# First projection of a hybrid decoder layer: four weight units run side by side by k tiles, weights fetched by pairs of k tiles, squares on ScalarE, and constant matmuls on TensorE before the input arrives

## The chip, the core and the metric

One core of one Trainium2 chip runs the whole kernel in one launch. The engines are named as the profile names them: PE is TensorE's matmul and PEld its weight load, DVE is VectorE, ACT is ScalarE, POOL is GpSimd, and SP is SyncE, which here only issues transfers. The metric is device microseconds (us) of one execution, as the median of several.

## What is computed

One decoder layer over 512 positions of width 1024. The part that the change touches is the start: the RMS norm of x and the first quarter of the combined input projection, the forget logits of the HGRN2 heads (512 columns, four heads of 128).

```python
h = rms_norm(x, norm_mix[l])            # x is (1, 512, 1024) f32
proj = h @ w_in[l]                      # (1024, 3584) weights
hq, hf, hi, hg, mq, mk, mv = jnp.split(proj, IN_SPLITS, axis=-1)
o_hgrn = hgrn2_mixer(hq, hf, hi, hg, lb_table[l], hgrn_norm[l])
# in it: f = lb + (1 - lb) * sigmoid(hf); log f is summed along chunks of 32 positions
```

After it come block-sparse attention, the output projection, cross-attention, a squared-ReLU MLP and a final norm.

## The kernel before, in words

**Precision.** Every operand of a large product is split in two: ACT copies it to a rounded part (`hi`, type fp32r), DVE subtracts that from the original (`lo`), and PE adds three products, hi·hi, hi·lo and lo·hi. A weight of 128 x 1024 values is a unit: `wr` is its raw tile (three buffers), `wh` and `wl` its two parts (`split_raw`, line 246). x is held transposed, as eight k tiles of 128 rows by 512 positions: `xraw` raw, `xhi` and `xlo` the parts, scaled by the norm's gain from `vec` (`split_x`, line 494). The division by the root of the mean square comes later: DVE and ACT square and add the k tiles (`square_x`, line 503, tiles `xsq`, `Sx`, `Sy`), PE sums that over partitions (`nr`), and ACT makes `rb1` of it, by which the finished products are multiplied.

**Tiling of the first projection.** Units 0 to 3 are the four heads of hf; a unit holds all eight k tiles of one head. PE (lines 595 to 610) goes through the k tiles once for heads 0 and 1 together (48 matmuls of 128 x 512), then once for head 2 and once for head 3 (24 each). So the first pass needs a new k tile of x every six matmuls, and the two weights whole. Each head has an accumulator bank from the pool `pacc` of four banks; another pool, `pside`, has four for everything else.

**What sets the order.** Down to line 607 each engine's instructions stand as the code writes them (`manual_schedule`); behind it the framework's scheduler places them, and side work (the norm's column sums `nc`, the HGRN2 steps) is put between matmuls by a planner, `Pace` (line 37), that adds up assumed costs. `need(u)` (line 315) splits units two ahead of use and loads them up to six ahead, as raw buffers come free.

**Queues.** SP issues the transfers of x and the weights one after the other; `vec` goes over ACT's queue. A transfer's issue waits when the eighth one before it has not landed, since eight semaphores are used in turn.

**What follows.** Stage hi (units 4 to 7, token by token, `tm_stage`) uses x again and all four banks of `pacc`; then come hq (units 8 to 11) and the HGRN2 work. `ev_f` (line 588) takes hf out of its banks with rb1, sigmoids follow, then the logarithm `lnf`, its chunk sums `b` (a scan on DVE), and their exponentials `eb` and `kt` on ACT. `Vh` is hi scaled, on ACT; it frees the banks that hq takes.

Of the kernel before, what the change touches and what calls it, by code (L numbers as in the profile page):

```python
# [122 lines left out]
def hybrid_layer(ctx: ExitStack, tc: tile.TileContext, xT, memT, ws, vecs, consts, rots, out):  # L123
    nc = tc.nc
    pace = Pace()
    V, A, PE = (pace.engine(e, t) for e, t in ((nc.vector, "dve"), (nc.scalar, "act"), (nc.tensor, "pe")))
    SY, PO = pace.engine(nc.sync, "dma"), pace.engine(nc.gpsimd, "pool")
# [8 lines left out]
    ordered = tc.manual_schedule()  # L136
# [33 lines left out]
    raws, his, los, late, n8 = {}, {}, {}, [], [1]  # L170
    state = {"load": 0, "split": 0}
# [74 lines left out]
    def split_raw(u, raw, a, b, eng=None):  # L246
        A.activation(his[u][:, a:b], raw[:, a:b], AF.Copy)

        def lower(hi=his[u], lo=los[u]):
            (eng or V).tensor_sub(lo[:, a:b], raw[:, a:b], hi[:, a:b].bitcast(F32))  # L250
        later(lower)

    def split_part(u, a, b, eng=None):
        split_raw(u, raws[u], a, b, eng)

    def split_begin():
        u = state["split"]
        his[u] = wpool.tile([P, D], F32R, tag="whi", name=f"wh{u}", bufs=WBUFS)
        if u < MLP - 4 and u % 4 == 0:
            los[u] = ep.tile([P, D], F32R, tag="wloe", name=f"wl{u}", bufs=1)  # L260
        else:
            los[u] = wpool.tile([P, D], F32R, tag="wlo", name=f"wl{u}", bufs=WBUFS - 1)
        state["split"] += 1
        return u

    def split_unit(eng=None):
        u = split_begin()
        split_part(u, 0, D, eng)
        del raws[u]
# [18 lines left out]
    def f1_prep(j, s):  # L288

        split_raw(split_begin(), f1raw[("ABCAcDd" if j == 7 else "ABDCAcD")[s], j], 0, D)  # L290
        if s == 1:
            f1_add(j, "A", "B", "C")
        if j == 7:
            if s == 1:
                f1_load(j, "d")
                state["load"] = FF2
            elif s > 2:
                load_unit()
            if s == 3:
                f1_add(j, "d", "d", "A")  # L300
        elif s == 1:
            f1_load(j + 1, "B")
        elif s == 2:
            f1_load(j + 1, "A")
        elif s == 3:
            f1_add(j, "D", "D", "A")
            f1_load(j + 1, "C")
        elif s == 5:
            f1_load(j + 1, "c")
        elif s == 6:  # L310
            f1_load(j + 1, "D")
        if s in (2, 6):
            more_sums()

    def need(u):
        marks.append(last_mm[0])
        if MLP <= u + SPLIT_AHEAD < FF2:
            f1_prep(*divmod(u + SPLIT_AHEAD - MLP, 7))
            return
        last = MLP if u < MLP else UNITS  # L320
        most = RAWS if u < MLP else 2 * RAWS
        want_load, want_split = min(last, u + LOAD_AHEAD + 1), min(last, u + SPLIT_AHEAD + 1)
        while state["split"] < want_split or state["load"] < want_load:
            if state["load"] < want_load and state["load"] - state["split"] < most:
                load_unit()
            elif state["split"] < want_split:
                split_unit()
            else:
                break
        if MLP - 6 <= u < MLP - 2:  # L330
            for what in ("A", "B", "CD", "c")[u - MLP + 6]:
                f1_load(0, what)
# [3 lines left out]

    side = []
    made = {}
    GAP, SLACK, NORM_AT = 4, 2.5, 6
    since = [0]  # L340
    last_mm = [None]

# [43 lines left out]
    def mm(o, l, r, start, stop):  # L386
        last_mm[0] = PE.matmul(o, l, r, start=start, stop=stop, skip_group_check=True)
        since[0] += 1
        if since[0] >= GAP:
            pump()  # L390

    def fm_k(u, acc, act, k, first, last, o=slice(None)):
        hi, lo = his[u], los[u]
        a_hi, a_lo = act(k)
        a_hi, a_lo = a_hi[:, o], a_lo[:, o]
        w_hi, w_lo = hi[:, k * P:(k + 1) * P], lo[:, k * P:(k + 1) * P]
        mm(acc, w_hi, a_hi, first, False)
        mm(acc, w_hi, a_lo, False, False)
        mm(acc, w_lo, a_hi, False, last)
# [46 lines left out]
    vec = cpool.tile([P, V_END], F32, name="vec")  # L446
# [6 lines left out]
    ones = cpool.tile([P, P], F32, name="ones")  # L453
# [6 lines left out]
    def load_x(k):  # L460
        SY.dma_start(xraw[k // 4][:, k % 4, :], xT[:, k])

    A.dma_start(vec, vecs)
    load_x(0)
    load_unit(((0, 2 * P),))
    load_unit(((0, D // 2),))
    load_x(1)
    SY.dma_start(raws[0][:, 2 * P:], ws[0][:, 2 * P:])
    load_x(2)
    SY.dma_start(raws[1][:, D // 2:], ws[1][:, D // 2:])  # L470
    for k in range(3, KT):
        load_x(k)
    nc.gpsimd.memset(eps, EPS)
    nc.gpsimd.memset(ones, 1.0)
    make_identity(nc, ident)
    nc.gpsimd.tensor_copy(ones_r, ones)
    ATs = []
    for i in range(2):
        t = ep.tile([P, NT, P], F32, name=f"AT{i}")
# [14 lines left out]
    def split_x(k):  # L494
        split_act(xhi[k // 4][:, k % 4, :], xlo[k // 4][:, k % 4, :], xraw[k // 4][:, k % 4, :], G_MIX, k)
# [7 lines left out]
    def square_x(k):  # L503
        q = sums.get(k) or s2(F32, f"xsq{k}")
        src = xraw[k // 4][:, k % 4, :]
        if k % 2 == 0:
            A.activation(q, src, AF.Square)
        else:
            V.tensor_mul(q, src, src)
        if k not in sums:  # L510
            S, eng = (Sx, V) if k < 4 else (Sy, V)
            eng.tensor_add(S, S, q)
        if k == KT - 1:
            V.tensor_add(Sx, Sx, Sy)

    split_begin()
    split_begin()
    split_x(0)
    split_part(0, 0, 2 * P)
    split_part(1, 0, D // 2)  # L520
    split_x(1)
    split_part(0, 2 * P, D, V)
    split_x(2)
    square_x(0)
    split_x(3)
    split_part(1, D // 2, D, V)
    square_x(1)
    del raws[0], raws[1]
    load_unit()
    load_unit()  # L530
    for k in range(4, KT):
        split_x(k)
        square_x(k - 2)
        if k == 6:
            split_unit(V)
    square_x(KT - 2)
    square_x(KT - 1)
    A.dma_start(cst, consts)
    A.dma_start(cmask[:, T - P:], consts[:, C_MASK:C_MASK + P])
    A.dma_start(rot, rots)  # L540
# [31 lines left out]
    x_act = pair(xhi, xlo)  # L572
# [4 lines left out]
    def lower_bounds():  # L577
        l0, l1 = vec[:, V_LB:V_LB + 4], vec[:, V_LB + 4:V_LB + 8]
        V.tensor_max(lb, l0, l1)
        V.tensor_sub(le0, l0, lb)  # L580
        V.tensor_sub(le1, l1, lb)
        A.activation(lbv[:, 2:4, :], lbv[:, 2:4, :], AF.Exp)
        V.tensor_add(le1, le0, le1)
        V.reciprocal(le1, le1)
        V.tensor_mul(lb, le0, le1)
        V.tensor_scalar(oml, lb, -1.0, 1.0, op0=ALU.mult, op1=ALU.add)
# [5 lines left out]
        V.tensor_scalar(f, f, oml[:, h:h + 1], lb[:, h:h + 1], op0=ALU.mult, op1=ALU.add)  # L592


    accs = [acc_bank(f"hf{j}") for j in range(HEADS)]
    for k in range(KT):
        for j in range(2):
            fm_k(j, accs[j], x_act, k, k == 0, k == KT - 1)
    split_unit()
    norm_x = norm_rows(Sx, T, rb1, rc1)  # L600
    next(norm_x)
    for k in range(KT):
        fm_k(2, accs[2], x_act, k, k == 0, k == KT - 1)
        if k == NORM_AT:
            next(norm_x)
    lower_bounds()
    ordered.__exit__(None, None, None)
    need(3)
    for k in range(KT):
        fm_k(3, accs[3], x_act, k, k == 0, k == KT - 1)  # L610
    for h in range(HEADS):
        ev_f(h, accs[h])
    start(norm_x, "nx", 1.0)
# [602 lines left out]
    ordered = tc.manual_schedule()  # L1216
# [77 lines left out]
    accs = {name: banks4(name) for name in "YX"}  # L1294
    for p, (name, begins, after) in enumerate(PLAN):
# [3 lines left out]
        for j in range(8):  # L1299
            i, c, n = 8 * p + j, j // 4, j % 4  # L1300
# [6 lines left out]
            hi, lo = his[FF2 + i], los[FF2 + i]  # L1307
# [86 lines left out]
```

## Time and profile before

| | |
|---|---|
| time, median of 3 runs | 747.05 us (746.96 to 747.32) |
| the profiled execution | 747.39 us, of which the span from the first to the last instruction is 745.6 us |
| mean granted TensorE clock over the span | 0.996 |
| PE busy, PEld busy | 728.1 us (98%), 636.2 us (85%) |
| DVE, ACT, POOL busy | 553.9 us, 415.4 us, 49.5 us |
| first matmul of hf, first of hi, first of hq | 6.14, 32.78, 55.65 us from the span's start |

The span is shorter than the time by 1.8 us, which lie outside what the profile records. In the trace a matmul's duration is longer than its turn on the engine, since matmuls are pipelined: the turn is the distance from one start to the next. An instruction's bracket says how long its engine was idle before it and what ended that. A transfer has two times: when a queue issued it, and when it landed.

### The profile page before, as it was taken

How to read it: one execution, taken by the hardware profiler on the slowest of the kernel's cores; microseconds unless marked ns; L12 is line 12 of the kernel's file. 1: busy time of each engine (PE TensorE's matmuls, PEld its weight loads, DVE VectorE, ACT ScalarE, POOL GpSimd, SP SyncE). 2: the span in 40 equal slices, each digit the busy share in tenths (PEclk: the TensorE clock that was granted, in tenths of full speed). 3: DMA queues.
4: the chain of work that ended last, by engine and by line, in shares of the span. 5: the costliest groups of instructions: out<-in, count | busy, mean ns of one | idle time of the engine just before them, and what ended most of it. 6: DMA issues, size and time to landing. Idle time of an engine off the chain costs nothing.

```text
span 745.6 us, 11110 instructions
## 1 busy us (share of the span) xinstructions
PE 728.1 (98%) x4248; PEld 636.2 (85%) x4248; DVE 553.9 (74%) x907; ACT 415.4 (56%) x634; POOL 49.5 (7%) x62
## 2 busy tenths in 40 slices
PE   6999999999999999999999999999999999999995
PEld 4888888777777898888888999999999888888884
DVE  5888554877766655777468788787888899987875
ACT  6673357434855454455356655555556654547662
POOL 1000000000011110012001011132110000000000
PEclk9999999999999999999999999999999999999998
DMA  8425334544589898459836398889995655546622
GB/s 277 144 84 165 116 113 123 167 136 138 163 200 251 204 271 326 142 117 259 280 113 151 98 254 217 232 197 237 244 225 204 211 185 193 174 163 205 198 91 79
DMA packets 44438, 136.97 MB, mean 184 GB/s; under 512 B 4545, under 2 KB 6977, under 8 KB 43745
## 3 DMA queue, kind: packets, MB, share of 16 engines
q1 hardware_dynamic: 34944, 110.64, 43.4%
q0 software_dynamic: 8960, 25.17, 19.0%
q8 instruction: 33, 0.54, 0.3%
q10 hardware_dynamic: 480, 0.45, 0.2%
q14 instruction: 21, 0.16, 0.1%
HBM read 134.15 MB, written 35.65 MB: 228 GB/s over the span
## 4 chain that ended last, share of the span: by engine, by line
PE 94%; DVE 2%; DMA 1%; ACT 1%; issue 1%; DVEq 0%; ACTq 0%
PE X L115 23%; PE Y L115 19%; PE xo L115 7%; PE mkq L115 6%; PE xq L115 6%; PE wo L115 5%; PE hg L115 3%; PE mv L115 3%; PE memv L115 3%; PE hq L115 3%; PE hi L115 3%; PE memk L115 2%; PE hf L115 2%; PE xs L115 2%; PE a L115 1%; PE sc L115 1%
## 5 line engine op out<-in xcount | busy, mean ns | idle before, releaser
L115 ACT ACTIVATE wh<-wr 128x1024 fp32r<-128x1024 f32 (+2 forms) x126 | 130.3, 1041 | 118.8 <-PE wo L115 19.6
L115 DVE TENSOR_TENSOR wl<-wr,wh 128x1024 fp32r<-128x1024 f32 (+2 forms) x126 | 151.2, 1204 | 33.6 <-ACT wh L115 23.3
L115 PE MATMUL X<-op,wh 128*128 128x512 f32 x256 | 90.6, 398 | 0.3 <-DVE x L115 0.3
L115 PE MATMUL X<-op,wl 128*128 128x256 f32 x256 | 72.3, 283 | 0.0
L115 PE MATMUL Y<-op,wh 128*128 128x512 f32 x192 | 68.0, 399 | 0.0
L115 PEld LDWEIGHTS X<-op,wh 128*128 128x128 f32 x256 | 48.1, 188 | 12.1 <-issue 0.5
L115 PE MATMUL Y<-op,wl 128*128 128x256 f32 x192 | 53.9, 281 | 0.0
L200 POOL DMA_DIRECT2D u<-in_ws_dram x32 | 31.0, 968 | 328.7 <-PE hg L115 201.3
L115 PEld LDWEIGHTS X<-op,wl 128*128 128x128 f32 x256 | 48.4, 189 | 0.3 <-DVE wl L115 0.2
L115 PE MATMUL Y<-OS,wh 128*128 128x256 f32 x256 | 47.2, 284 | 0.2 <-ACT t L115 0.2
L115 PE MATMUL X<-OS,wh 128*128 128x256 f32 x256 | 46.5, 283 | 0.0
L115 PEld LDWEIGHTS Y<-op,wh 128*128 128x128 f32 x192 | 36.1, 188 | 9.0
L115 PEld LDWEIGHTS Y<-OS,wh 128*128 128x128 f32 x256 | 39.9, 192 | 0.5 <-ACT t L115 0.4
L115 PEld LDWEIGHTS X<-OS,wh 128*128 128x128 f32 x256 | 39.9, 192 | 0.0
L115 PEld LDWEIGHTS Y<-op,wl 128*128 128x128 f32 x192 | 36.3, 189 | 0.0
L115 PE MATMUL X<-OS,wl 128*128 128x256 f32 x128 | 36.2, 283 | 0.0
L115 PE MATMUL Y<-OS,wl 128*128 128x256 f32 x128 | 36.2, 283 | 0.0
L115 ACT ACTIVATE g<-t 128x512 f32<-128x512 f32 x32 | 19.0, 625 | 30.2 <-DVE t L115 30.2
L115 DVE TENSOR_TENSOR op<-g,op 128x1024 fp32r<-128x1024 f32 x24 | 29.3, 1220 | 2.8 <-ACT op L115 2.8
L115 ACT ACTIVATE op<-g 128x1024 fp32r<-128x1024 f32 x28 | 29.2, 1044 | 0.5 <-PE X L115 0.5
L115 ACT ACT_TABLE_LOAD x22 | 28.2, 1283 | 1.6 <-PEq L1382 1.2
L115 PE MATMUL mkq<-xhi,wh 128*128 128x512 f32 x64 | 26.7, 417 | 0.0
(307 smaller groups left out, 2028.8 us busy)
## 6 DMA issues: line engine op xcount, KB each, us to landing
wr<-in_ws_dram SPq DMA_DIRECT2D x90, 512.0 KB, 4.4
u<-in_ws_dram POOLq DMA_DIRECT2D x32, 512.0 KB, 7.6
wr<-u SPq DMA_DIRECT2D x32, 512.0 KB, 3.3
u<-in_ws_dram SPq DMA_DIRECT2D x16, 512.0 KB, 4.1
u<-u SPq DMA_DIRECT2D x16, 512.0 KB, 5.3
wA<-in_ws_dram SPq DMA_DIRECT2D x8, 512.0 KB, 5.6
wD<-in_ws_dram SPq DMA_DIRECT2D x8, 512.0 KB, 6.7
wB<-in_ws_dram SPq DMA_DIRECT2D x8, 512.0 KB, 3.6
```

What stands on the lines that cost most here:

```text
L115: return f(*args, **kw)
L200: return nc.gpsimd.dma_start(dst, src, accum_op=ALU.add, max_dma_last_dim=4 * D)
```

## The change

The four units of hf are no longer one head each. New unit v holds k tiles 2v and 2v+1 of all four heads (view `by_k`), so its transfer gathers runs of 1 KB in DRAM, where it had runs of 1, 2, 3 or 4 KB; unit 0 comes in three pieces with runs of 512 bytes. PE goes through the k tiles once, with twelve matmuls on each, three for each of the four heads. Heads 2 and 3 take their banks from `pside`. Eleven matmuls of a 128 x 128 tile of ones, in plain f32, stand ahead of it on PE and write a bank that nobody reads. All eight squares are on ACT. `vec` moves to SP's queue, and the first two weight pieces to ACT's. The norm's sums on PE stand ahead of the last k tile.

```diff
-    A.dma_start(vec, vecs)
+    SY.dma_start(vec, vecs)
     load_x(0)
-    load_unit(((0, 2 * P),))
-    load_unit(((0, D // 2),))
+    load_first(0, 0, slice(0, 2), A)
+    load_first(0, 0, slice(2, 4), A)
     load_x(1)
-    SY.dma_start(raws[0][:, 2 * P:], ws[0][:, 2 * P:])
+    load_first(0, 1)
     load_x(2)
-    SY.dma_start(raws[1][:, D // 2:], ws[1][:, D // 2:])
-    for k in range(3, KT):
+    load_first(1)
+    load_x(3)
+    load_x(4)
+    load_first(2)
+    for k in range(5, KT):
         load_x(k)
...
-        if k % 2 == 0:
-            A.activation(q, src, AF.Square)
-        else:
-            V.tensor_mul(q, src, src)
+        A.activation(q, src, AF.Square)
...
+    warm = side_bank("warm")
+    for i in range(WARM):
+        PE.matmul(warm[:, :P], ones, ones, start=True, stop=True, skip_group_check=True)
...
-    accs = [acc_bank(f"hf{j}") for j in range(HEADS)]
-    for k in range(KT):
-        for j in range(2):
-            fm_k(j, accs[j], x_act, k, k == 0, k == KT - 1)
-    split_unit()
+    accs = [(acc_bank if j < 2 else side_bank)(f"hf{j}") for j in range(HEADS)]
     norm_x = norm_rows(Sx, T, rb1, rc1)
     next(norm_x)
     for k in range(KT):
-        fm_k(2, accs[2], x_act, k, k == 0, k == KT - 1)
-        if k == NORM_AT:
+        if k % 2 == 0:
+            need(k // 2)
+        if k == KT - 1:
             next(norm_x)
-    lower_bounds()
-    ordered.__exit__(None, None, None)
-    need(3)
-    for k in range(KT):
-        fm_k(3, accs[3], x_act, k, k == 0, k == KT - 1)
+            lower_bounds()
+            ordered.__exit__(None, None, None)
+        a_hi, a_lo = x_act(k)
+        for hs in ((0, 1), (2, 3)) if k == 0 else ((0,), (1,), (2,), (3,)):
+            w = {h: [by_k(t[k // 2])[:, h, k % 2] for t in (his, los)] for h in hs}
+            for h in hs:
+                mm(accs[h], w[h][0], a_hi, k == 0, False)
+            for h in hs:
+                mm(accs[h], w[h][1], a_hi, False, False)
+            for h in hs:
+                mm(accs[h], w[h][0], a_lo, False, k == KT - 1)
```

The new loads and splits of the first units:

```python
def load_first(v, k=None, h=slice(None), eng=None):   # WARM is 11
    ...
    src = ws[h if h != slice(None) else slice(0, HEADS)].rearrange("h p c -> p h c")
    if k is None:
        (eng or SY).dma_start(raws[v].rearrange("p (h c) -> p h c", h=HEADS), src[:, :, 2 * v * P:(2 * v + 2) * P])
    else:
        (eng or SY).dma_start(by_k(raws[v])[:, h, k], src[:, :, (2 * v + k) * P:(2 * v + k + 1) * P])
```

**PE, the program's first rows.** Before, and then after; hf0 to hf3 are the four heads' banks, and the number behind the underscore only tells buffers apart.

```order
L115 MATMUL hf0_221<-xhi0_121,wh0_157 128x512
L115 MATMUL hf0_221<-xlo0_123,wh0_157 128x512
L115 MATMUL hf0_221<-xhi0_121,wl0_158 128x512
L115 MATMUL hf1_222<-xhi0_121,wh1_159 128x512
L115 MATMUL hf1_222<-xlo0_123,wh1_159 128x512
L115 MATMUL hf1_222<-xhi0_121,wl1_160 128x512
```

```order
L115 MATMUL warm_159<-ones_116 128x128 x11
L115 MATMUL hf0_237<-xhi0_121,wh0_171 128x512
L115 MATMUL hf1_238<-xhi0_121,wh0_171 128x512
L115 MATMUL hf0_237<-xhi0_121,wl0_172 128x512
L115 MATMUL hf1_238<-xhi0_121,wl0_172 128x512
L115 MATMUL hf0_237<-xlo0_123,wh0_171 128x512
L115 MATMUL hf1_238<-xlo0_123,wh0_171 128x512
L115 MATMUL hf2_239<-xhi0_121,wh0_171 128x512
```

The second matmul wanted `xlo` and now wants only `xhi`; `xlo` is first used by the fifth matmul of hf.

**ACT, the program's start.** Before, and then after; `sink` is a one-column warm-up of the table, `Sx` and `xsq` are squares.

```order
L115 DMA vec_109<-in_vecs_dram 128x52
L115 ACT_TABLE_LOAD
L115 ACTIVATE sink_114<-eps_115 128x1
L115 ACTIVATE xhi0_121<-xraw0_119,vec_109 128x512
L115 ACTIVATE wh0_157<-wr0_127 128x256
L115 ACTIVATE wh1_159<-wr1_129 128x512
L115 ACTIVATE xhi0_121<-xraw0_119,vec_109 128x512
L115 ACTIVATE wh0_157<-wr0_127 128x768
```

```order
L115 DMA wr0_127<-in_ws_dram 128x2x128 x2
L115 ACT_TABLE_LOAD
L115 ACTIVATE sink_114<-eps_115 128x1
L115 ACTIVATE wh0_171<-wr0_127 128x2x128
L115 ACTIVATE xhi0_121<-xraw0_119,vec_109 128x512
L115 ACTIVATE wh0_171<-wr0_127 128x2x128
L115 ACTIVATE xhi0_121<-xraw0_119,vec_109 128x512
L115 ACTIVATE wh0_171<-wr0_127 128x4x128
L115 ACTIVATE xhi0_121<-xraw0_119,vec_109 128x512
L115 ACTIVATE wh1_187<-wr1_133 128x1024
```

The first weight piece is now split ahead of the first k tile of x, and the weights for a k tile stand next to that tile.

**ACT at the end of stage hi.** Before, and then after; the Vh rows free the banks that hq takes, `b_553` and `b_550` are the scan of the third head.

```order
L115 ACTIVATE wh10_607<-wr10_478 128x1024
L115 ACTIVATE Vh_373<-hi0_377,rc1_218 128x512
L115 ACTIVATE eb2_555<-b_553 128x512
L115 ACTIVATE kt2_556<-b_553 128x512
L115 ACTIVATE lnf_375<-lnf_375 128x512
```

```order
L115 ACTIVATE wh10_613<-wr10_451 128x1024
L115 ACTIVATE eb2_552<-b_550 128x512
L115 ACTIVATE kt2_553<-b_550 128x512
L115 ACTIVATE Vh_385<-hi0_389,rc1_234 128x512
L115 ACTIVATE lnf_387<-lnf_387 128x512
```

Two exponentials of the third head, which wait for a scan on DVE, have moved ahead of the first Vh.

## Rows read from the trace of the kernel before

**Rows 1.** The page: PE's busy time and its share, its busy tenths in 40 slices, and the engines' shares of the chain that ended last.

```profile
PE 728.1 (98%) x4248; PEld 636.2 (85%) x4248; DVE 553.9 (74%) x907; ACT 415.4 (56%) x634; POOL 49.5 (7%) x62
...
PE   6999999999999999999999999999999999999995
...
PE 94%; DVE 2%; DMA 1%; ACT 1%; issue 1%; DVEq 0%; ACTq 0%
```

**Rows 2.** The chain that ended last, in order of time, over the first 80 us: start, length, what.

```profile
5.05 5.82 DMA xraw<-in_xT_dram
...
20.10 6.20 PE hf L115 x26
26.30 0.48 PE nr L115 x2
26.78 6.17 PE hf L115 x27
...
55.65 15.42 PE hq L115 x68
```

**Rows 3.** PE's timeline from the first matmul to the first of stage hi: start, duration, operation, and in brackets the idle time before it. Between the first and second row lie 7 more matmuls, between the second and the row at 20.10 34.

```profile
6.14 0.79 PE L115 MATMUL hf<-xhi,wh 128*128 128x512 f32 x1 [6.14 <-ACT wh L115]
...
9.89 0.39 PE L115 MATMUL hf<-xhi,wl 128*128 128x512 f32 x1
...
14.04 0.39 PE L115 MATMUL hf<-xhi,wh 128*128 128x512 f32 x1
15.05 0.50 PE L115 MATMUL hf<-xlo,wh 128*128 128x512 f32 x1 [0.63 <-DVE xlo L115]
...
18.30 0.50 PE L115 MATMUL hf<-xlo,wh 128*128 128x512 f32 x1 [0.24 <-DVE xlo L115]
...
20.10 0.50 PE L115 MATMUL hf<-xlo,wh 128*128 128x512 f32 x1
...
32.78 0.39 PE L115 MATMUL hi<-wh,xhi 128*128 128x512 f32 x1
```

**Rows 4.** Stretches of the start: the last columns are the granted clock, the mean busy share of the 16 DMA engines and GB/s.

```profile
0.00:2.00 2.00, 0.00 (x0) 0.00 (x0) 0.00 (x0) 0.82 (x1) 1.39 (x10) 1.00 0.18 17
2.00:3.00 1.00, 0.00 (x0) 0.00 (x0) 0.00 (x0) 0.67 (x2) 1.00 (x3) 1.00 1.03 218
3.00:4.00 1.00, 0.00 (x0) 0.00 (x0) 0.00 (x0) 0.00 (x0) 0.58 (x3) 1.00 0.50 159
4.00:5.00 1.00, 0.00 (x0) 0.00 (x0) 0.00 (x0) 0.00 (x0) 0.00 (x0) 1.00 0.86 232
...
10.00:14.00 4.00, 3.79 (x17) 2.81 (x16) 3.67 (x6) 3.95 (x8) 0.00 (x0) 1.00 1.04 402
```

**Rows 5.** The splits of x, its squares, and the splits of weights, by tile: duration in ns least, median and most, first and last start.

```profile
L115 ACT ACTIVATE xhi<-xraw,vec x8: 707/710/722, 5.1 to 15.9; 128x512 fp32r<-128x512 f32 x8
L115 DVE SCALAR_TENSOR_TENSOR xlo<-xraw,vec,xhi x8: 743/746/754, 5.8 to 19.3; 128x512 fp32r<-128x512 f32 x8
L115 DVE TENSOR_TENSOR xsq<-xraw x4: 683/684/686, 12.9 to 22.1; 128x512 f32<-128x512 f32 x4
L115 ACT ACTIVATE xsq<-xraw x2: 613/614/614, 12.7 to 16.5; 128x512 f32<-128x512 f32 x2
...
L115 ACT ACTIVATE wh<-wr x11: 398/1042/1061, 5.7 to 39.4; 128x1024 fp32r<-128x1024 f32 x7, 128x512 fp32r<-128x512 f32 x2, 128x256 fp32r<-128x256 f32 x1, 128x768 fp32r<-128x768 f32 x1
L115 DVE TENSOR_TENSOR wl<-wr,wh x10: 418/1218/1225, 6.5 to 35.0; 128x1024 fp32r<-128x1024 f32 x6, 128x512 fp32r<-128x512 f32 x2, 128x256 fp32r<-128x256 f32 x1, 128x768 fp32r<-128x768 f32 x1
```

**Rows 6.** Single transfers by the moment of issue, with the us from issue to landing in the last column: x's first tile and vec (issued at 0.74 and 0.73), the first weight piece (1.18), the second (1.6), x's second tile (2.12), the first whole unit (8.86).

```profile
xraw<-in_xT_dram SPq DMA_DIRECT2D x1, 256.0 KB, 4.1
vec<-in_vecs_dram ACTq DMA_DIRECT2D x1, 26.0 KB, 4.3
...
wr<-in_ws_dram SPq DMA_DIRECT2D x1, 128.0 KB, 4.0
...
wr<-in_ws_dram SPq DMA_DIRECT2D x1, 256.0 KB, 5.2
...
xraw<-in_xT_dram SPq DMA_DIRECT2D x1, 256.0 KB, 5.7
...
wr<-in_ws_dram SPq DMA_DIRECT2D x1, 512.0 KB, 6.0
```

**Rows 7.** SP's queue, first 12 us: start and length of the issue.

```profile
0.74 0.39 SPq L115 DMA_DIRECT2D xraw<-in_xT_dram  x1
1.18 0.90 SPq L115 DMA_DIRECT2D wr<-in_ws_dram  x2
2.12 0.43 SPq L115 DMA_DIRECT2D xraw<-in_xT_dram  x1
...
8.86 2.20 SPq L115 DMA_DIRECT2D wr<-in_ws_dram  x2
```

**Rows 8.** The chain that ended last, at 72 us: plain f32 matmuls of 128 x 128. The profile records each of them twice.

```profile
72.34 0.89 PE a L115 x8
```

**Rows 9.** ACT's and DVE's timelines: the step that makes rb1, and, at the end of stage hi, the scans of the third and fourth head and the first exponential that waits for them.

```profile
28.82 0.63 ACT L115 ACTIVATE rb<-rb 128x512 f32<-128x512 f32 x1
...
51.77 2.33 DVE L115 TENSOR_TENSOR_SCAN b<-scan_mask,lnf 128x512 f32<-128x512 f32 x2
...
53.03 0.63 ACT L115 ACTIVATE eb<-b 128x512 f32<-128x512 f32 x1 [0.73 <-DVE b L115]
```

More of the change, by code (lines that the diff above doesn't have):

```diff
@@ L338, in hybrid_layer @@
     made = {}
-    GAP, SLACK, NORM_AT = 4, 2.5, 6
+    GAP, SLACK, WARM = 4, 2.5, 11
     since = [0]
@@ L461, in load_x, with by_k, split_first @@
         SY.dma_start(xraw[k // 4][:, k % 4, :], xT[:, k])
-    A.dma_start(vec, vecs)
+    def by_k(t):
+        return t.rearrange("p (h k c) -> p h k c", h=HEADS, k=2)
+    def load_first(v, k=None, h=slice(None), eng=None):
+        if v not in raws:
+            raws[v] = raw_tile(f"wr{v}", False)
+            state["load"] += 1
+        src = ws[h if h != slice(None) else slice(0, HEADS)].rearrange("h p c -> p h c")
+        if k is None:
+            (eng or SY).dma_start(raws[v].rearrange("p (h c) -> p h c", h=HEADS), src[:, :, 2 * v * P:(2 * v + 2) * P])
+        else:
+            (eng or SY).dma_start(by_k(raws[v])[:, h, k], src[:, :, (2 * v + k) * P:(2 * v + k + 1) * P])
+    def split_first(v, k, h=slice(None)):
+        hi, lo, raw = (by_k(t)[:, h, k] for t in (his[v], los[v], raws[v]))
+        A.activation(hi, raw, AF.Copy)
+        V.tensor_sub(lo, raw, hi.bitcast(F32))
+    SY.dma_start(vec, vecs)
     load_x(0)
-    load_unit(((0, 2 * P),))
-    load_unit(((0, D // 2),))
+    load_first(0, 0, slice(0, 2), A)
+    load_first(0, 0, slice(2, 4), A)
     load_x(1)
-    SY.dma_start(raws[0][:, 2 * P:], ws[0][:, 2 * P:])
+    load_first(0, 1)
     load_x(2)
-    SY.dma_start(raws[1][:, D // 2:], ws[1][:, D // 2:])
-    for k in range(3, KT):
+    load_first(1)
[3 more added lines that the diff above has]
+    for k in range(5, KT):
         load_x(k)
+    nc.gpsimd.memset(ones, 1.0)
     nc.gpsimd.memset(eps, EPS)
-    nc.gpsimd.memset(ones, 1.0)
     make_identity(nc, ident)
@@ L514, in square_x @@
             V.tensor_add(Sx, Sx, Sy)
+    warm = side_bank("warm")
+    for i in range(WARM):
+        PE.matmul(warm[:, :P], ones, ones, start=True, stop=True, skip_group_check=True)
     split_begin()
-    split_begin()
+    split_first(0, 0, slice(0, 2))
     split_x(0)
-    split_part(0, 0, 2 * P)
-    split_part(1, 0, D // 2)
+    split_first(0, 0, slice(2, 4))
     split_x(1)
-    split_part(0, 2 * P, D, V)
+    split_first(0, 1)
+    load_first(3)
     split_x(2)
+    split_unit()
     square_x(0)
     split_x(3)
-    split_part(1, D // 2, D, V)
     square_x(1)
[L528 to L537, printed above, removed]
+    split_x(4)
+    split_unit()
+    square_x(2)
+    split_x(5)
+    square_x(3)
+    split_x(6)
+    split_unit()
+    square_x(4)
+    split_x(7)
+    for k in range(5, KT):
+        square_x(k)
+    del raws[0]
     A.dma_start(cst, consts)
```

## The prediction

> **What bounds the kernel now.** I read the page first. PE is busy 98% of the span and makes 94% of the chain that ended last; only the first of its 40 slices stands at 6 tenths [rows 1]. So PE bounds the kernel nearly everywhere, and a change to the start can win only what PE loses at the start; what it wins there reaches the end if no other engine falls behind later. The chain says where PE is not the bound: until 20.10 it leads over transfers, ACT and DVE, and from 20.10 on over PE alone, through hf, nr, hi and hq [rows 2].
>
> PE's timeline splits the stage. The rate is 27 matmuls in 6.17 us, 0.2285 us each [rows 2]. From 6.14 to 9.89 there are eight turns in 3.75 us, 0.47 us each [rows 3]. A turn of 512 columns at 1.2 GHz is 0.43 us and at 2.4 GHz 0.21 us, so PE was at the lower level until about 9.9, 3.75 us after its first matmul. (The clock column shows 1.00 there already [rows 4]; I go by the spacing.) At full rate the eight take 1.83 us: 1.92 us lost. From 9.89 to 20.10 there are 35 turns in 10.21 us; at full rate 8.00 us: 2.21 us lost, in waits for the lower part of x, as the gap from 14.04 to 15.05 and the brackets show [rows 3]. From 20.10 to 32.78, 55 turns take 12.68 us against 12.57: nothing to win. The stage therefore holds 1.92 + 2.21 + 0.1 = 4.2 us, more or less by as much as the first matmul moves.
>
> **The change, part by part.** PE keeps the 96 matmuls of hf and the two of nr, 98 x 0.2285 = 22.4 us at full rate. What changes is when it starts and what it waits for.
>
> *The first matmul* needs the first weight piece split, which ACT now does first, and `xhi` of tile 0: the tile landed, 0.71 us on ACT [rows 5] and two handovers of some 0.04 us. Before, vec landed last, at 0.73 + 4.3 = 5.03, and x's tile at 0.74 + 4.1 = 4.84 [rows 6]. Now vec, the tile and both weight pieces of 128 KB are under way together, 538 KB, where 410 KB were (without the second piece). Lower bound: the tile is only issued one issue later, 0.44 us [rows 7], and lands at 5.3. Upper bound: the transfer that brought the sum to 666 KB landed at 1.6 + 5.2 = 6.8 [rows 6]. In between: the stretches moved 0.41 MB by 4.0 us and 0.64 MB by 5.0 [rows 4]; so 410 KB (0.42 MB) were moved at 4.05 and had landed at 1.18 + 4.0 = 5.2, that is 1.15 later, and 538 KB (0.55 MB) were moved at 4.6, which gives a landing at 5.75. I take that, as it rests on the same bytes on the same DMA engines: first matmul at 5.75 + 0.8 = 6.55, say 6.6 (bounds 6.1 and 7.6), 0.45 us later than before.
>
> The second queue does not help here. On ACT's queue 26 KB of vec took 4.3 us beside 256 KB on SP's that took 4.1 [rows 6]: the two were served together. The Trainium skill (DMA: Bandwidth & Descriptors, "Issuing engines are not separate DMA queues") says that transfers issued by different engines run on the same DMA engines and interleave, and only the time to issue is saved. These rows agree with it; if the queues were separate, x's tile would land at 5.3, and the first matmul would come 0.45 us sooner.
>
> *The warm matmuls.* Eight records in 0.89 us are four plain f32 matmuls of 128 x 128, 0.22 us each [rows 8]; at half the clock 0.44, and eleven 4.9 us. They wait for the tile of ones, which POOL writes within its first microsecond, so they end at about 5.9, ahead of 6.6, and cost nothing, even with x at its lower bound. The trace of before has no such prelude, so what it does to the clock is bounded from both sides. If the clock rises 3.75 us after PE's first matmul as it did, that is at 4.7, and all of hf runs at 2.4 GHz. If constants don't count, it rises at 6.6 + 3.75, and eight turns are slow again. I take the first: when the clock rose before, PE was doing nothing but matmuls one behind the other [rows 3], and so it is now. The 1.92 us are then won.
>
> *Waits for data.* From the second tile of x (922 KB in all, landed at 2.12 + 5.7 = 7.8) to the first whole unit (3610 KB, at 8.86 + 6.0 = 14.86) data came at 382 KB per us [rows 6, 7]. Now the pieces for k tile 1 are in at 1050 KB, 8.15, and unit 1 at 1818 KB, 10.2. Runs of 512 bytes and 1 KB may come more slowly than those of 2 KB and more that made 402 GB/s; the nearest rows below are the stretches of 159 to 232 GB/s, in which vec's runs of 208 bytes are about [rows 4]. Nearer to the first, I allow 0.25 us for the one and 0.4 for the other. Then, with a split of 512 columns at 0.61 us on ACT and 0.69 on DVE (estimates between the 256 and the 1024 columns of [rows 5]), k tile 1's lower part is there at 9.7, while PE wants it at 6.6 + 13 x 0.2285 = 9.55: a wait of 0.2. Unit 1 is split at 10.6 + 1.04 + 1.22 = 12.9; PE wants it at 12.5: a wait of 0.4. Each wait costs 0.1 more in restarting, as the longer turn at 15.05 shows [rows 3]. In all 0.8 us. From then on a k tile takes PE 12 x 0.2285 = 2.74 us, while DVE has for it 0.75 for xlo, 0.61 for half a unit and some 0.69 for one sum, 2.0 us, and ACT 0.71 + 0.52 + 0.61 = 1.9 us [rows 5]; data come every 1.35 us. So PE does not wait again. Before, the first pass took a k tile every 6 x 0.2285 = 1.37 us, which DVE could not follow. The four squares that move from DVE to ACT lie under this cover; left on DVE they would make it 2.4 us a k tile, still below 2.74.
>
> *The norm.* nr stands ahead of the last k tile, at 6.6 + 84 x 0.2285 + 0.8 = 26.6. DVE's work up to `nrl` adds up to 16 us from 6.6 on (eight times 0.75, four units, eight sums); with ACT's rounding of the sum and some waits it ends at 23 to 24.5: no wait.
>
> *Sum.* Stage hi starts at 6.6 + 22.4 + 0.8 = 29.8 instead of 32.78: 3.0 us sooner.
>
> **What follows hi.** All four heads end together, and are taken out of their banks later relative to PE. hi's third token group needs the first head's bank at 29.8 + 12 x 0.2285 = 32.5. rb1 was there at 28.82 + 0.63 = 29.45, 3.15 after nr's first matmul [rows 2, 9]; now it is there at 29.8, and the first bank is free one DVE step of 0.7 us later, 2 us early. At the end of hi, the first Vh now stands behind two exponentials of the third head, which wait for DVE's scan, and hq waits for the bank. hq comes at 55.65 - 3.0 = 52.65. If the scan kept its old time of 51.77, its exponential would start at 53.03 [rows 9] and Vh would end three ACT steps of 0.6 later, at 54.8: 2.2 us of wait. But DVE's chain hangs on hf's end, which moves by 3.0, and one weight split of 1.22 us fewer stands ahead of that scan; against that, the four evacuations and sigmoids now come in a row behind rb1, up to 2 us. So the scan comes at 47.6 to 49.6, and Vh ends at 50.6 to 52.6: just in time. PE's waits further on are short, and what they wait for follows PE. I cost it at nothing and keep 2.2 us for the range. The profiled execution would take 747.39 - 3.0 = 744.4 us, 0.34 above the median as before, and the median 747.05 - 3.0 = 744.05; I say 744.0.
>
> **Rivals.**
> - *The clock is late*: the prelude doesn't lift it, or it falls again in the 0.7 us without work before x. Eight slow turns lose 1.92 us, of which the wait of 0.4 for unit 1 is absorbed: gain 1.5, time 745.5. For it: no row shows such a prelude. Against it: a wait of 0.63 us did not lower the clock before [rows 3]. The Trainium skill (TensorE: Matmul & The Clock Gate, "Part 1") says that one kernel began with 6, 11 or 14 slow matmuls in different runs; no run here shows that.
> - *The HGRN2 chain becomes the bound* at the end of hi, as worked out: 2.2 us given back, time 746.2.
> - *Slower: short runs choke the start.* The gain is gone when unit 1's lower part comes 3.0 + 0.5 us later than 12.9, that is, when the first 1818 KB have landed at 14.1 instead of 10.6. From 2 us, when data start, and less the 1.15 us to landing, that is 1.86 MB in 10.95 us, 170 GB/s, where the trace has 159 to 232 GB/s while vec's short runs are about, and 402 without. At 159 they land at 14.9: 0.8 us worse than before, and units 2 and 3 come as slowly; time 749. Against it: vec's runs are less than half as long as the shortest new ones.
> - *The change does nothing*: waits on `xlo` stay, since ACT now does all squares and splits. Time 747. Against it: 1.9 us of ACT work in 2.74.
>
> **How the numbers follow.** Forecast 0.78, with its own range from 742.7 (x at the lower bound and no waits: hi at 6.1 + 22.4 = 28.5, 4.3 us sooner) to 745.1 (x at the upper bound and the waits kept: 30.8, 2.0 sooner). Late clock 0.08, HGRN2 chain 0.05, nothing 0.05, slower 0.04. The range runs from 742.7 to 745.8 and takes in the late clock; 0.14 is left out above, a little below. A measurement of this kernel can tell about 0.2%, 1.5 us, so faster means below 745.55: the forecast and half of the late clock, 0.82; within 0.2%, the other half and the next two, 0.14; slower 0.04.
>
> **What would show it.** First hf matmul at 6.1 to 7.6; turns of 0.23 us from the first on (if they are 0.43, the step on the clock is wrong); one or two waits on `wl` in k tiles 1 and 2 and none on `xlo` after; hi's first matmul at 28.5 to 30.8; hq's 22.9 us after it (if more, the chain of Vh is at fault); from there the same distances as before. The prediction is wrong if hi starts 3 us sooner and the end does not move, or if unit 1 lands after 13 us.

## The result and the profile after

| | median, us | lowest to highest | runs |
|---|---|---|---|
| before | 747.05 | 746.91 to 747.36 | 5 |
| changed | 743.16 | 742.79 to 743.73 | 5 |

The ratio is 0.9947, with a 95% interval from 0.9933 to 0.9960: the change wins 3.9 us, between 3.0 and 5.0. Forecast were 3.0 us (744.0). The changed kernel's profiled execution is its longest: 743.73 us for a span of 742.0. The other four have spans of 741.0 to 741.5. A second execution (the experiment "once more", 742.84 us, span 741.1) is therefore shown beside it where the two differ.

On the page, PE's first slice now stands at 9 where it stood at 6 [rows 1]; this is largely the matmuls on constants, so it is no measure of the gain.

```profile
PE   9999999999999999999999999999999999999995
```

The chain that ended last, of the first 80 us of the first execution (start us, us, what), is PE alone from 0.99 on, where before it led over transfers, ACT and DVE until 20.10 [rows 2]:

```profile
0.99 5.06 PE warm L115 x22
6.05 19.49 PE hf L115 x84
25.55 0.48 PE nr L115 x2
```

In the second execution the chain still leads over x's first transfer (1.18 to 4.84) and its split, and over PE alone from 5.71 on: there the constants' matmuls end before x is ready.

PE's timeline of the first execution (start us, us, engine, line, operation, tiles, shapes, count):

```profile
0.99 5.06 PE L115 MATMUL warm<-ones 128*128 128x128 f32 x22 [0.99 <-POOL eps L496]
5.77 1.16 PE L115 MATMUL hf<-xhi,wh 128*128 128x512 f32 x2
6.76 0.63 PE L115 MATMUL hf<-xhi,wl 128*128 128x512 f32 x2
...
28.63 0.39 PE L115 MATMUL hi<-wh,xhi 128*128 128x512 f32 x1
...
51.34 0.39 PE L115 MATMUL hq<-xhi,wh 128*128 128x512 f32 x1
```

and of the second:

```profile
0.99 4.38 PE L115 MATMUL warm<-ones 128*128 128x128 f32 x22 [0.99 <-POOL eps L496]
5.71 0.73 PE L115 MATMUL hf<-xhi,wh 128*128 128x512 f32 x2 [0.34 <-ACT xhi L115]
6.28 0.62 PE L115 MATMUL hf<-xhi,wl 128*128 128x512 f32 x2
...
28.19 0.39 PE L115 MATMUL hi<-wh,xhi 128*128 128x512 f32 x1
...
50.90 0.39 PE L115 MATMUL hq<-xhi,wh 128*128 128x512 f32 x1
```

Read the starts, not the durations. Before, eight turns took 0.47 us each [rows 3]. In the first execution two turns take 0.99 us and all others 0.23; in the second all take 0.23 to 0.29. Neither timeline shows the waits on `xlo` that stood at 15.05 before. Stage hi starts at 28.63 and at 28.19 instead of 32.78 [rows 3], 4.15 and 4.59 us sooner.

The times of the data explain why no wait is left. ACT's timeline and DVE's, of the first execution:

```profile
5.00 0.72 ACT L115 ACTIVATE xhi<-xraw,vec 128x512 fp32r<-128x512 f32 x1 [1.37 <-DMA xraw<-in_xT_dram]
...
9.23 1.06 ACT L115 ACTIVATE wh<-wr 128x1024 fp32r<-128x1024 f32 x1 [0.92 <-DMA wr<-in_ws_dram]
```

```profile
10.33 1.22 DVE L115 TENSOR_TENSOR wl<-wr,wh 128x1024 fp32r<-128x1024 f32 x1 [1.23 <-ACT wh L115]
...
22.71 0.69 DVE L115 TENSOR_TENSOR nrl<-Sx,nrh 128x512 fp32r<-128x512 f32 x1 [0.70 <-ACT nrh L115]
```

Transfers of the first 10 us of that execution (tile, queue, count, KB each, median us from issue to landing); vec took 4.3 us before [rows 6]:

```profile
wr<-in_ws_dram ACTq DMA_DIRECT2D x2, 128.0 KB, 3.3
wr<-in_ws_dram SPq DMA_DIRECT2D x1, 256.0 KB, 4.8
vec<-in_vecs_dram SPq DMA_DIRECT2D x1, 26.0 KB, 2.1
```

Windows of the core (us, PE, PEld, DVE, ACT and POOL busy, granted clock, DMA share, GB/s):

```profile
2.00:3.00 1.00, 1.00 (x6) 1.00 (x6) 0.00 (x0) 1.00 (x1) 1.00 (x3) 1.00 0.96 229
3.00:4.00 1.00, 1.00 (x7) 1.00 (x6) 0.34 (x1) 0.62 (x3) 0.57 (x3) 1.00 0.95 159
4.00:5.00 1.00, 1.00 (x7) 1.00 (x7) 0.09 (x1) 0.00 (x1) 0.00 (x0) 1.00 1.01 304
...
10.00:14.00 4.00, 4.00 (x19) 3.34 (x18) 3.61 (x5) 4.00 (x8) 0.00 (x0) 1.00 1.07 369
```

Behind hi the distances stay: hq follows it after 22.71 us in both executions, as in the kernel before, whose timeline has hi at 32.78 and hq at 55.49 (the 55.65 given ahead for hq is where the chain's piece starts):

```profile
55.49 0.39 PE L115 MATMUL hq<-xhi,wh 128*128 128x512 f32 x1
```

In the first execution some 0.45 us is given back shortly after wo starts at 202.16. The chain that ended last runs there from the transfer of `mraw` over ACT's and DVE's splits of it to PE:

```profile
191.80 8.40 DMA mraw<-in_memT_dram
...
208.16 17.05 PE wo L115 x74
```

In the second that transfer took 7.9 us and nothing is given back: its span is 4.5 us shorter than that of the kernel before, as its hi starts 4.59 sooner.

### The profile page after: what moved, and what is told of

Its sections match the earlier page's. It is cut to its first block, busy times and chain, and to the rows that moved or that the text cites. A ratio compares the mean times of both kernels' runs of the same rounds, so it can differ in the third digit from the quotient of the medians.

```text
span 742.0 us, 11155 instructions
## 1 busy us (share of the span) xinstructions
PE 730.6 (98%) x4270; PEld 640.9 (86%) x4270; DVE 551.8 (74%) x903; ACT 417.5 (56%) x638; POOL 49.4 (7%) x62
## 4 chain that ended last, share of the span: by engine, by line
PE 93%; DVE 3%; ACT 1%; DMA 1%; issue 1%; DVEq 0%; POOL 0%; SPq 0%; ACTq 0%; POOLq 0%
PE X L115 23%; PE Y L115 19%; PE xo L115 7%; PE mkq L115 6%; PE xq L115 6%; PE wo L115 5%; PE hf L115 3%; PE mv L115 3%; PE memv L115 3%; PE hq L115 3%; PE hi L115 3%; PE memk L115 2%; PE xs L115 2%; PE hg L115 1%; PE a L115 1%; DMA mraw<-in_memT_dram 1%
```

## The experiments

Eleven runs, each compared with the kernel before on its chip (747.08 to 747.12 there). Times below stand against the changed kernel's 743.16 and, in the repetition, 742.9. All compute the whole reference.

### Once more

The changed kernel unedited.

> The changed kernel once more, unedited, for a second profile of it. Its first profile had PE's clock up at 6.5 (22 halves of the constants' matmuls in 5.06 us, two slow turns of hf), hi at 28.63, and lost 0.45 us at wo's start, where the transfer of mraw took 8.4 us (7.6 to 7.9 in the kernel before and in three of its variants). Theory: both are chance and change from one execution to the next: if the clock is up at about 4.2 to 4.7, as in one variant with the same constants, hi comes at 28.0 to 28.2; mraw lands in 7.6 to 7.9 us and wo loses nothing; time 742.8 to 743.3. Rival: both belong to the kernel: hi at 28.6, wo 0.4 late again, time 743.2 to 743.7.

Measured: 742.9 us (742.82 to 743.25), ratio 0.9945 [0.9933, 0.9958]. The rows are shown above. The 22 halves of the constants' matmuls take 4.38 us instead of 5.06. A half takes 0.23 us at 1.2 GHz and 0.115 at 2.4, so six were at the higher clock, and it rose at about 4.7. The first theory holds: the late clock and the wait at wo belong to that execution and not to every execution of the kernel.

### No matmuls on constants

```diff
-    GAP, SLACK, WARM = 4, 2.5, 11
+    GAP, SLACK, WARM = 4, 2.5, 0
```

> The changed kernel without its eleven matmuls on constants. Changed kernel: 743.16 us, first hf matmul 5.77, two slow turns (0.99 us for both), hi at 28.63. My theory: the matmuls on constants count for the clock, and without them PE's first eight turns of hf take 3.75 us as in the kernel before, instead of 0.99 for two and 6 x 0.2285 for the rest (2.36): 1.4 us lost, hi at 30.0, time 744.55. Rival: what was won is the order and the earlier data, and the clock rises at 6.5 whatever PE did (or a later PE finds its data waiting and loses nothing): hi at 28.6 to 28.8, time 743.2.

Measured: 745.0 us (744.39 to 745.45), ratio 0.9972 [0.9960, 0.9983]. PE's timeline of the profiled execution (the shortest of the six):

```profile
5.76 1.22 PE L115 MATMUL hf<-xhi,wh 128*128 128x512 f32 x2 [5.76 <-ACT xhi L115]
...
7.63 1.05 PE L115 MATMUL hf<-xlo,wh 128*128 128x512 f32 x2
8.48 0.90 PE L115 MATMUL hf<-xhi,wh 128*128 128x512 f32 x2
9.22 0.63 PE L115 MATMUL hf<-xhi,wl 128*128 128x512 f32 x2
```

The first matmul comes at the same time, and seven turns take 0.43 to 0.5 us: the first six in 2.72, the next two together in 0.74. hi comes 1.1 us later than in the first execution of the changed kernel and 1.6 later than in the second; the medians differ by 1.8 to 2.1. The matmuls on constants are worth about the 1.92 us that I gave them, and the rival falls.

### The same matmuls ahead of the kernel before

On POOL the tile of ones is also written first.

```diff
+    warm = side_bank("warm")
+    for i in range(11):
+        PE.matmul(warm[:, :P], ones, ones, start=True, stop=True, skip_group_check=True)
     split_begin()
```

> The kernel before with the eleven matmuls on constants put ahead of hf (ones set first on POOL), nothing else. Theory: its first pass is fed by DVE's lower parts of x, so the 1.9 us that eight fast turns win come back as waits on xlo and on the second half of the weights; the pass ends at 20.1 as before, time 746.8 to 747.1. Rival: the clock is a term of its own, and the 1.9 us reach the end: hi at 30.9, time 745.1.

Measured: 747.27 us (746.76 to 748.21), ratio 1.0002 [0.9993, 1.0011]: nothing. Its waits of PE in the first 34 us (waited for, us in total, times, longest) are:

```profile
PE hf L115 <- DVE xlo L115: 1.5, 4, 0.6
```

The turns are quick from the start wherever the data are there, and PE stands four times waiting for DVE. In this execution hi starts at 32.32, 0.46 sooner than before, but so do the data: vec landed 0.4 us sooner, and DVE's last `xlo` started at 18.85 instead of 19.30. That lead is still there at hq and gone at the end; where it goes is not shown. The clock is no term of its own: it is worth 1.9 us only where the order lets PE go on.

### The old order of the heads in the changed kernel

Everything of the change but the order: heads 0 and 1 over all k tiles, then 2 and 3.

```diff
-    for k in range(KT):
+    for hp in ((0, 1), (2, 3)):
+        for k in range(KT):
...
-        for hs in ((0, 1), (2, 3)) if k == 0 else ((0,), (1,), (2,), (3,)):
+            for hs in (hp,) if k == 0 else ((hp[0],), (hp[1],)):
```

> The changed kernel with its loads, splits, squares and matmuls on constants, but heads 0 and 1 over all eight k tiles first and heads 2 and 3 after, as in the kernel before. My theory: DVE, not the data, sets the first pass (a k tile takes it 2.0 us, PE 1.37): its lower part of the last k tile ends at 19.1 whatever PE does, so the first pass ends at 19.6 to 20.0; then 48 matmuls of 0.2285 and 0.5 for nr: hi at 31.1 to 31.5 instead of 28.63, 2.5 to 2.9 us lost, time 745.7 to 746.0. Rival: the gain is the earlier data and the clock, the order of the heads is worth nothing: hi at 28.6 to 29.0, time 743.2.

Measured: 747.64 us (747.35 to 747.99), ratio 1.0008 [0.9999, 1.0017]; hi at 32.56. PE's timeline:

```profile
10.39 0.49 PE L115 MATMUL hf<-xhi,wh 128*128 128x512 f32 x1 [0.75 <-ACT wh L115]
11.65 0.50 PE L115 MATMUL hf<-xhi,wl 128*128 128x512 f32 x1 [0.77 <-DVE wl L115]
...
18.53 0.50 PE L115 MATMUL hf<-xhi,wl 128*128 128x512 f32 x1 [0.63 <-DVE wl L115]
...
32.56 0.39 PE L115 MATMUL hi<-wh,xhi 128*128 128x512 f32 x1
```

The theory has the mechanism and undersized it. I counted on the lower part of x's last tile at 19.1; but the last unit's `wl`, wanted one k tile earlier in PE's order, is written from 17.26 to 18.49, and eleven turns hang on it. With the longer first one they end at 21.16, and 11.0 + 0.5 more are 32.6. With the warm clock and the early data, but without the order, the whole gain is gone. The 4.5 us is not the worth of the order alone: the splits still follow the new loads, so DVE splits heads 2 and 3 in the first pass too, where nothing uses them yet.

### vec at the head of ACT's queue again

```diff
-    SY.dma_start(vec, vecs)
+    A.dma_start(vec, vecs)
```

> The changed kernel with vec's transfer back at the head of ACT's queue, ahead of the two weight pieces there, so that x's first tile heads SP's queue. Changed kernel: vec 0.74 to 2.8, x's tile 1.19 to 4.9. Theory A, that vec's 128 runs of 208 bytes are slow only while they share the DMA engines with other transfers, and that heading SP's queue let them through alone: vec lands at 5.0 or later, as it did in the kernel before (0.73 + 4.3), x's tile at 4.9 to 5.8, first hf matmul at 5.9 to 6.6, time 743.2 to 743.9. Rival B, that the bytes ahead decide and the place doesn't: vec at about 2.8, x's tile 0.45 sooner at 4.45, first hf matmul held by the matmuls on constants until 5.77, time 743.1. Rival C, the queue of ACT itself is slower to start: weight pieces land later by one issue (3.6 instead of 3.2) and vec at 2.8: first matmul unchanged.

Measured: 744.11 us (743.82 to 744.23), ratio 0.9959 [0.9947, 0.9972]; first hf matmul at 6.66, hi at 29.11. ACT's timeline:

```profile
0.73 0.41 ACTq L115 DMA_DIRECT2D vec<-in_vecs_dram  x1
1.18 0.98 ACTq L115 DMA_DIRECT2D wr<-in_ws_dram  x2
...
5.58 0.42 ACT L115 ACTIVATE wh<-wr 128x256 fp32r<-128x256 f32 x1 [1.90 <-DMA wr<-in_ws_dram]
5.90 0.70 ACT L115 ACTIVATE xhi<-xraw,vec 128x512 fp32r<-128x512 f32 x1
```

Two transfers of that execution, by what they brought (us from issue at 0.74 and 0.73 to landing in the last column):

```profile
xraw<-in_xT_dram SPq DMA_DIRECT2D x1, 256.0 KB, 3.6
vec<-in_vecs_dram ACTq DMA_DIRECT2D x1, 26.0 KB, 3.8
```

vec takes 3.8 us instead of 2.1, so its place matters, as theory A says, and rival B is wrong there. But vec lands at 4.5, not at 5.0 or later, and x's tile at 4.3, where B had it, half a microsecond sooner than in the changed kernel; the time lies above A's range. It is neither of them that PE waits for. The first weight piece, behind vec on the same queue, lands at 5.56, 4.4 us after its issue, instead of at 3.2; ACT splits it ahead of x, and so x's split comes at 5.90. That is C's place with a size nobody gave it. So vec's new queue is worth about 1 us by what stands behind it. Whether the queue itself or the transfers beside it make the difference is not separated: with vec, x's tile changes its place too.

### The squares back on DVE

```diff
-        A.activation(q, src, AF.Square)
+        if k % 2 == 0:
+            A.activation(q, src, AF.Square)
+        else:
+            V.tensor_mul(q, src, src)
```

> The changed kernel with the squares of the odd k tiles back on DVE. The prediction counted this at nothing, as DVE's 2.4 us a k tile stay below PE's 2.74: time 743.2, nr at 25.38 as now. Rival, by the trace of the changed kernel: DVE is busy without a gap from 10.33 to 22.0, and the lower part that nr needs is written at 23.40 where nr wants it at 25.38; four squares of 0.69 us more end it at 26.1, so nr and what stands behind it wait 0.7 us: hi at 29.4, time 743.9.

Measured: 744.13 us (743.78 to 744.60), ratio 0.9961 [0.9947, 0.9975]. PE's timeline:

```profile
25.34 0.47 PE L115 MATMUL nr<-nrh,ones_r 128*128 128x512 f32 x1
25.97 0.50 PE L115 MATMUL nr<-nrl,ones_r 128*128 128x512 f32 x1 [0.16 <-DVE nrl L115]
```

nr's second matmul stands until 25.92, when its lower part is written: the first has a turn of 0.63 us instead of 0.24. hi starts at 29.05, 0.42 us later than in the first execution of the changed kernel and 0.86 later than in the second. By the medians it is 1.0 us; this execution is the shortest of its five, and what the longer ones lose is not shown. The rival's mechanism holds, and its 0.7 lies between these figures; the prediction's zero is wrong.

### Three parts undone at once

No matmuls on constants, vec on ACT's queue, squares on DVE (the three edits above together); the order stays.

> The changed kernel with three of its parts undone at once: no matmuls on constants, vec back at the head of ACT's queue, squares of the odd k tiles back on DVE; the order of loads and matmuls side by side stays. Alone each of the three cost 0.95 to 1.8 us and the order 4.5, 8.2 in all where the whole change gained 3.9, so they can't add. Theory: they lie beside each other: first hf matmul at 6.7, eight slow turns (1.9 us), 84 turns: nr wanted at 27.7, where DVE's 26.0 no longer makes it wait; hi at 30.9 to 31.0, time 745.5 to 745.9. Rival: they add on the path, 0.95 + 1.8 + 0.97 above 743.0: 746.8.

Measured: 745.9 us (745.13 to 747.34), ratio 0.9985 [0.9976, 0.9994]. First hf matmul 6.73; in the profiled execution (746.68) the first fourteen turns are slow, 6.14 us in all, as the starts show (12 matmuls lie between the two rows):

```profile
6.73 1.22 PE L115 MATMUL hf<-xhi,wh 128*128 128x512 f32 x2 [6.73 <-ACT xhi L115]
...
12.87 0.43 PE L115 MATMUL hf<-xlo,wh 128*128 128x512 f32 x1
```

The median is at the end of the theory's range, 2.7 us above the changed kernel's 743.16, where the three parts alone make 1.84 + 0.95 + 0.97 = 3.76. The squares cost nothing any more, since PE comes to nr only at 28.78 in this execution, after its lower part was written at 26.0. The order alone wins 1.2 us here, and the three others need it to win theirs. The executions spread by 2.2 us. The clock may be why: it rose 6.1 us after PE's first matmul in this one, and after 3.2 in the traced one without constants above; for the others it is not shown.

### Six matmuls on constants

`WARM = 6`.

> The changed kernel with six matmuls on constants instead of eleven: they end at about 3.75, and PE has nothing to do until x's tile is there at 5.7. Theory A: the clock only rises when PE's work goes on without such a break; the first turns of hf are slow as they are without constants: hi at 29.7, time 744.6 to 745.0. Rival B: what counts is the time since PE's first matmul, and a break of 2 us does no harm: clock up at 4.2 to 6.5 as with eleven, hi at 28.0 to 28.6, time 743.2.

Measured: 744.5 us (742.97, 743.34, 744.50, 745.28 and 745.73), ratio 0.9963 [0.9951, 0.9976]. In the profiled one (745.73):

```profile
0.99 2.93 PE L115 MATMUL warm<-ones 128*128 128x128 f32 x12 [0.99 <-POOL eps L496]
5.98 1.22 PE L115 MATMUL hf<-xhi,wh 128*128 128x512 f32 x2 [2.06 <-ACT xhi L115]
...
11.27 0.57 PE L115 MATMUL hf<-xhi,wh 128*128 128x512 f32 x1
```

Neither theory is right as it stood. Two executions are as quick as with eleven, and this one, after a break of 2.06 us, has twelve slow turns, between the seven and the fourteen of the two traces without any prelude above. The prelude that ended early left the time uncertain; the one that lasts until x is there kept ten executions within 1 us (742.79 to 743.73).

### The second weight piece behind x on SP's queue

```diff
-    load_first(0, 0, slice(2, 4), A)
+    load_first(0, 0, slice(2, 4))
```

> The changed kernel with the second weight piece (heads 2 and 3 of k tile 0, 128 KB) on SP's queue behind x's first tile instead of on ACT's queue beside it. Theory, the prediction's rule by bytes: 410 KB instead of 538 are under way up to x's landing, 0.3 to 0.5 us less: x lands at 4.4 to 4.6, first hf matmul at 5.2 to 5.4 if the clock is up by then; but unit 1 lands no sooner than 9.2 and its lower part is written at 11.5, where PE then wants it at 11.0, so the gain is eaten there: time 743.0 to 743.3. Rival: x's landing isn't set by what is beside it: x at 4.9, first hf matmul at 5.7, time 743.2.

Measured: 744.95 us (744.52 to 746.35), ratio 0.9970 [0.9958, 0.9982]. Both theories miss the time. PE's timeline of the longest execution, and two of its windows:

```profile
5.16 0.73 PE L115 MATMUL hf<-xhi,wh 128*128 128x512 f32 x2
...
9.86 0.50 PE L115 MATMUL hf<-xhi,wh 128*128 128x512 f32 x1 [1.68 <-ACT wh L115]
10.59 0.69 PE L115 MATMUL hf<-xhi,wl 128*128 128x512 f32 x1 [0.22 <-DVE wl L115]
11.07 0.63 PE L115 MATMUL hf<-xlo,wh 128*128 128x512 f32 x1
...
14.05 0.45 PE L115 MATMUL hf<-xhi,wh 128*128 128x512 f32 x1
```

```profile
5.00:6.00 1.00, 0.93 (x5) 0.70 (x5) 0.85 (x2) 0.53 (x2) 0.00 (x0) 1.00 0.55 112
...
10.00:14.00 4.00, 3.78 (x9) 2.78 (x10) 2.84 (x4) 3.24 (x6) 0.00 (x0) 0.59 1.07 376
```

x is split from 4.39 on and hf starts at 5.16, as the theory had it. But the piece of k tile 1 lands 6.5 us after its issue, at 9.2 instead of 6.9, behind a stretch in which the DMA engines stand at 0.55 and 112 GB/s though SP had issued four more transfers behind it by 5.4. PE waits 1.68 us, and after that its turns take 0.43 us and the granted clock of the stretch is 0.59. What held the transfers there is not shown. The other five executions are 0.8 us or more above every execution of the changed kernel as it is, so a loss is not one execution's chance, though their waits are not traced. Whether the clock falls in them too is not shown; their granted clock over the whole span, 0.996 to 0.998 against 0.993 in this one and 0.996 or 0.997 in the changed kernel, speaks against it.

### The second piece later on ACT's queue, and unit 1 ahead of x's third tile

Two kernels; the second has both edits.

```diff
-    load_first(0, 0, slice(2, 4), A)
...
     A.activation(sink, eps, AF.Ln)
+    load_first(0, 0, slice(2, 4), A)
```

```diff
-    load_x(2)
     load_first(1)
+    load_x(2)
...
-    split_x(2)
     split_unit()
+    split_x(2)
```

> The changed kernel with the second weight piece (heads 2 and 3 of k tile 0) still on ACT's queue, but issued after ACT's table load and first small step, at about 2.7 instead of 1.2, so that it is not beside x's first tile and the second queue is kept. Theory by bytes: x lands at 4.4 as it did with the piece on SP's queue, first hf matmul at 5.2 to 5.4 if the clock is up by then (up to 6.05 if it is late); the piece lands at about 6.0, is split at 6.9, and is wanted at 6.7 to 7.2; the next piece stays at 6.9; unit 1's lower part, written at 11.4, is now wanted at 11.1: 0.3 of the 0.4 us are eaten, hi at 28.0, time 742.7 to 743.1. Rival, that a queue with only long transfers ahead of short runs stalls as with the piece on SP's queue: k tile 1's piece at 9.2, time 744.7 to 745.

> As the one before, and unit 1 is loaded and split ahead of x's third tile instead of behind it. Theory: unit 1 lands 256 KB sooner, 0.7 us, at 8.4; its lower part is written at 10.7; x's third tile lands at 9.1 and its lower part is written at 11.4 where PE wants it at 11.1 to 11.3: waits 0.1 to 0.3, hi at 27.8 to 28.0, time 742.4 to 743.0. Rival: the wait only changes its name, time as the run before, 742.7 to 743.1.

Measured: 743.13 us (742.65 to 743.23), ratio 0.9945 [0.9933, 0.9957], and 743.02 us (742.90 to 743.24), ratio 0.9945 [0.9932, 0.9957]: neither can be told from the changed kernel. The first edit did not do what I wanted. ACT's rows show the piece issued while the table load runs, 0.1 us later than before:

```profile
1.23 1.28 ACT L115 ACT_TABLE_LOAD   x1 [1.23 <-PEq L1411]
1.29 0.42 ACTq L115 DMA_DIRECT2D wr<-in_ws_dram  x1
```

So it says nothing on the bytes beside x, and x's first split started at 4.47 in the one and at 5.09 in the other, with the same transfers ahead of it. The 4.39 of the experiment before lies just below that spread: whether the second piece slows x stays open. In the second kernel unit 1's split starts at 8.78 instead of 9.23 and 9.07, and nothing follows, as PE waited for it by less than 0.1 us in any of these traces. No version here beats the changed kernel.

## Why the prediction was right, and where its sizes were off

*The mechanism* is shown from both sides. With the old order the gain is gone (747.64) though all else is kept; the clock alone wins nothing (747.27); the order alone wins 1.2 us (745.9). What PE waited for was DVE in the first pass, and the remedy is that a k tile now gives PE 2.74 us of work for DVE's 2.0.

*The first matmul*, forecast at 6.6, came at 5.77 and 5.71: the forecast was some 0.85 us too late, and the measured times lie below its lower bound of 6.1. The step that failed is the landing of x's tile at 5.75 by the bytes under way; it landed at 4.9. The rate was near right: 0.55 MB were moved by 4.0 + 0.143 / 0.304 = 4.5 (forecast 4.6). The lag from there to the landing is 0.4, not the 1.15 that I read off the first weight piece of the kernel before. The lag is no constant that can be carried from one transfer to another: with vec back on ACT's queue the first weight piece landed at 5.56, some 1.5 after as many bytes had been moved (0.42 MB by 4.0), and x's tile already at 4.3. What sets it is not shown. The lower bound failed in the same way: it put x's landing one issue after the old one, at 5.3, and took the time from issue to landing as fixed (4.1 before, 3.7 now).

The Trainium skill (DMA: Bandwidth & Descriptors, "Issuing engines are not separate DMA queues") says that starting transfers from several engines saves only the time to issue them. Two edits that move one transfer to the other queue cost more than an issue of 0.44 us: vec's 0.95 us, the second weight piece's 1.8 us. That does not refute the page, since each edit also changes what stands ahead of and beside the other transfers; it does show that here a change of queue has another price than one issue.

The eleven constants fit just so: in the first execution PE passes from them to hf at 5.77 without a pause, 0.05 us after x's split ended at 5.72.

*The waits for data*, forecast at 0.8, are nil in the first execution and below 0.1 in the second. Unit 1 was split from 9.23 where I had it landing at 10.6, and its lower part was written at 11.55 where PE wanted it at 12.0. Short runs cost little: 369 GB/s in the stretch that made 402 before [rows 4], not the 159 of the slower rival.

*The clock*, forecast to rise 3.75 us after PE's first matmul, did so after 3.7 us in the second execution and after 5.5 in the first, where two turns cost 0.5. That is the late rival in a small part, and it lies between the ends that I gave. The Trainium skill (TensorE: Matmul & The Clock Gate, "Part 1") says that the number of slow first matmuls changes from run to run of one kernel; the rows agree, with two slow turns of hf in one execution and none in the other. The prediction names [rows 4] for the clock column in the slow turns of the kernel before, but these rows leave out 5 to 10 us; the column does stand at 1.00 there.

So the sum of 29.8 for hi becomes 28.63 by 0.83 (first matmul) and 0.8 (waits) less 0.5 (clock), and 28.19 by 0.89 and 0.8 less 0.1. The two large errors point the same way; in the first execution the late clock and the 0.45 us at wo make up for part of them, which is luck and not a merit of the sum.

*The squares* left on DVE I costed at nothing, and they cost 1.0 us by the medians, 0.4 to 0.9 by hi's start. I compared rates, DVE's 2.4 us a k tile with PE's 2.74, and didn't follow the end of DVE's row of work: with the four squares in it `nrl` is written at 25.92, behind the 25.4 at which PE comes to nr. With them on ACT it is written at 23.40, in the 23 to 24.5 that I gave.

*Behind hi* nothing was lost, as forecast: from hi to hq it stays at 22.71 us, and 4.5 of the 4.59 us reach the end in the second execution. The HGRN2 rival, the one of short runs and that of no change are out.

## What to carry to other kernels

A wait on a feeding engine is best removed by giving the bounding engine more work for each thing fed; a faster clock or an earlier start in front of such a wait only makes it longer. When an engine's share of a loop is compared with the bound's, look also at where its last result of the loop is wanted: the sum at the end can be late though every round fits. Try each part alone and all but each: here the parts, each undone alone, cost 8.2 us where the whole won 3.9, and the order was worth 4.5 us by the one way and 1.2 by the other.

## What the runs showed of the hardware

- The time from PE's first matmul to the higher clock differed between executions of almost the same start. With eleven matmuls on constants it was 3.1 us (second piece on SP's queue), 3.2 (old order), 3.7 and 5.5 (the changed kernel twice), and some 4.5 to 5.5 in the other traces with eleven; without them about 3.2 and 6.1; each from the spacing of turns or of the constants' halves. The clock column shows 1.00 throughout these stretches.
- After a wait of 1.68 us PE ran at 0.43 us a turn again, from 10.59 to 14.05, and there the column shows it, at 0.59. Waits of 0.63 us in the kernel before [rows 3] and of 0.75 and 0.77 with the old order did not do that.
- At the head of ACT's queue, with x's tile at the head of SP's, 26 KB in runs of 208 bytes took 3.8 to 4.3 us in four traces; at the head of SP's queue, with a weight piece at the head of ACT's, 2.1 us in all the others. That piece took 2.5 us at the head of ACT's queue and 4.4 behind vec. Why is not shown.
- A transfer written behind ACT's table load is issued while the load runs (1.29 against 1.23 to 2.51).
